# GLA state at token 256 in the lane of the levels, squares one step behind their matmuls, gate transfers tied to the second v product's first tile

## The chip, the cores and the metric

The kernel runs on one core of one Trainium2 chip. The metric is the device time of one execution in microseconds (us). The core has a matmul engine (TensorE, PE in the profile; PEld is its weight load), a vector engine (VectorE, DVE), a scalar engine (ScalarE, ACT), GpSimd (POOL) and SyncE (SP), which here only issues transfers. Each engine works through its own instructions in a fixed order; semaphores make one wait for another. Matmul results go to PSUM, in two pools of four banks here, called mm and px.

## The reference

One decoder layer on 512 tokens of width 1024, in float32: a layer norm; gated linear attention (GLA, 4 heads, keys of 128, values of 256) and latent attention side by side, each projected back; the two merged by sigmoid gates and projected; a norm; a squared-ReLU MLP of width 4096; a norm. The GLA part, which the change touches, is

```
q_g, k_g, v_g, r_g, a_lr, q_lat, kv_lat, gate_logits = jnp.split(h @ w_in, offsets, axis=-1)
log_a = jax.nn.log_sigmoid((a_lr @ w_gla_a2 + b_gla_a2).astype(jnp.float32)) / GLA_TAU
# S_t = diag(a_t) S_{t-1} + k_t^T v_t,  o_t = q_t S_t
o_gla = gla_chunked(q * GLA_HK ** -0.5, k, v, log_a)
o_gla = rms_norm(o_gla.transpose(0, 2, 1, 3), gla_norm_g.reshape(GLA_HEADS, GLA_HV))
y_gla = (o_gla * jax.nn.silu(r_g)) @ w_o_gla
g_gla, g_mla = jnp.split(jax.nn.sigmoid(gate_logits + b_gate), N_BRANCH, axis=-1)
return (g_gla * y_gla + g_mla * y_mla) @ w_out
```

## The kernel before

Every product in float32 is made of three matmuls: both operands are split into a high part (rounded, written by ACT) and a low part (the remainder, written by VectorE), and high x high, high x low and low x high are summed in PSUM. For weights the parts are whi and wlo, made by split (L191 on ACT, L192 on VectorE) from a tile of 512 KB. A tile comes in a buffer wraw (three of them, loaded on SP's queue at L176) or wq; whi and wlo have two buffers each. fetch, which issues L176, runs two tiles ahead of the products.

The products of the normed input run one after the other: q and k, v of heads 0 and 1 (proj_v(0)), r (proj_r, L752 to L754), v of heads 2 and 3 (proj_v(1), L281 to L283), then the gates (unit, L1222 to L1224). r and the gates use a scheme of fewer multiplications, for which some weight tiles are sums or differences of two source tiles: u_load issues one transfer on SP (L1195) and, for the sums, a second one on POOL (L1197) that adds to the tile where it lies. The first six gate tiles (wq of "g0": two each of "t1", "22", "t3") are called for ahead of proj_v(1). The gates also read shifted inputs sh (L1282, 16 transfers on SP).

Between the matmuls of these products runs the work of GLA, in generators (lanes) that a product moves on by a step at a time (tick). lane_levels runs gla_levels for head 0, 1, 2, 3. A head's scores are built level by level (blocks of 2, 4, ... 256 tokens): decays makes the decay factors dec (ACT L781 and L787) from sums gs that POOL makes (L785), M is packed by ACT (L811), L851, L867, L870 and L874 are its matmuls into px, and SD collects the scores; sd, s128 and s256 are the split results. lane_out runs gla_out for each head, once SS[h] (the levels), Vh[h] (the split v, vh and vl) and four blocks of r (rg) are there: first the state at token 256, the sum of k^T v over the first 256 tokens, six matmuls of 128x256 (L906 to L908), and its split over the same s256 tile; then for four blocks i of 128 tokens the output (L928 to L930): three matmuls for each of the terms, two blocks to a px bank; then the square of each block with its row sum (osq, gss; ACT L932), the root on POOL (grs L937), the scaling by rg (og L942) and transposes (L948).

The order that each engine gets is not the order of the code: a scheduler of the language works on recorded instructions (schedule_with_timeline_sim in L1693), and tc.issue_after tells it that instructions may stand only behind a given one. Names in the rows below are those of the program; a number behind a name tells one buffer from another.

Of the kernel before, what the change touches and what calls it, by code (L numbers as in the profile page):

```python
# [10 lines left out]
F32 = mybir.dt.float32  # L11
# [4 lines left out]
AF = mybir.ActivationFunctionType  # L16
# [3 lines left out]
P = 128  # L20
T = 512
D = 1024
NT = T // P
# [3 lines left out]
GH = 4  # L27
HV = 256
# [24 lines left out]
def tile_hybrid_block(ctx: ExitStack, tc: tile.TileContext, I, out, dbg=None):  # L53
    nc = tc.nc
# [11 lines left out]
    def nm(s):  # L66
        uid[0] += 1
        return f"{s}_{uid[0]}"
# [4 lines left out]
    def A(shape, dt=F32, n="a"):  # L73
        tag, bufs = ("C", 8) if n in TAG_C else (n, TAG_W[n]) if n in TAG_W else ("A", 24)
        return pa.tile(shape, dt, tag=tag, bufs=bufs, name=nm(n))

    def B(shape, dt=F32, n="b"):
        return pb.tile(shape, dt, tag="B", name=nm(n))

    def S(shape, dt=F32, n="s"):  # L80
        return sm.tile(shape, dt, tag=n, name=nm(n))
# [8 lines left out]
    def PX(shape=(P, T), dt=F32, n="px"):  # L90
        return px.tile(list(shape), dt, tag="px", name=nm(n))

    def f(ap):
        return ap.bitcast(F32)

    act = nc.scalar.activation
# [12 lines left out]
    def split(src, hi, lo, scale=None):  # L109
        if scale is None:  # L110
            act(hi, src, AF.Copy)
            return vtt(lo, src, f(hi), op=ALU.subtract)
        else:
            act(hi, src, AF.Copy, scale=scale)
            return stt(lo, src, scale, f(hi), op0=ALU.mult, op1=ALU.subtract)
# [23 lines left out]
    stream = []  # L139
# [24 lines left out]
    def fetch(n):  # L164
        while st["dma"] < min(len(stream), n):
            e = stream[st["dma"]]
            st["dma"] += 1
            if "src" in e:
                continue
            raw = A([P, e["nk"], T * 2 // e["nk"]], F32, "wraw")  # L170
            for sl, src, cw in e["dmas"]:
                if cw is None:
                    dst = raw[:, sl, :e["n"]]
                else:
                    dst = raw[:, sl[0], sl[1]].rearrange("p (h c) -> p h c", c=cw)
                nc.sync.dma_start(dst, src)  # L176
            e["raw"] = raw

    def pump(i):
# [122 lines left out]
    PL = {}  # L302
# [16 lines left out]
    for op, _ in RW:  # L319
        for hf in range(2):  # L320
            PL["r"].append(len(stream))
            e = {"nk": 2, "n": T, "res": False, "ahead": 2, "home": "wwwwrwrwrwwwrw"[2 * RW.index((op, _)) + hf]}
# [24 lines left out]
    def u_src(key, i, j, g):  # L347
        name, c0, gs = UNITS[key]
        src = I[name].rearrange("(k p) n -> p k n", p=P)
        c0 += (j * gs + g) * 256  # L350
        return src[:, i:8:2, c0:c0 + 256]
# [312 lines left out]
    Vh = [None] * GH  # L664
# [24 lines left out]
    rgn = [0] * GH  # L689
# [84 lines left out]
    SS = [None] * GH  # L774
# [119 lines left out]
        split(p[:, :256].rearrange("p (t i) -> p t i", i=P), sd[:, 0, 2:], sd[:, 1, 2:])  # L894
        SS[h] = (sd, s128, s256)

    def gla_out(h):
        while SS[h] is None or Vh[h] is None or rgn[h] < NT:
            yield
        sd, s128, s256 = SS[h]  # L900

        vh, vl = Vh[h]
        p = PX()[:, :HV]
        for j in range(2):
            kh, kl = [s256[:, 0, w, j * P:(j + 1) * P] for w in range(2)]
            mm(p, kh, vh[:, j, :], start=j == 0, stop=False)  # L906
            mm(p, kh, vl[:, j, :], start=False, stop=False)
            mm(p, kl, vh[:, j, :], start=False, stop=j == 1)  # L908
        sh, sl = s256[:, 0, 0], s256[:, 0, 1]
        split(p, sh, sl)  # L910

        def terms(i):
            if i % 2:
                yield (s128[:, 0, i // 2], s128[:, 1, i // 2]), (vh[:, i - 1, :], vl[:, i - 1, :])
            yield (sd[:, 0, i], sd[:, 1, i]), (vh[:, i, :], vl[:, i, :])
            if i >= 2:
                c = slice((i - 2) * P, (i - 1) * P)
                yield (s256[:, 1, 0, c], s256[:, 1, 1, c]), (sh, sl)

        ss = S([P, NT], F32, "gss")  # L920
        ps = []
        for i in range(NT):
            if i % 2 == 0:
                ps.append(PX())
            o = ps[i // 2][:, (i % 2) * HV:(i % 2 + 1) * HV]
            ts = list(terms(i))
            for n, ((ah, al), (wh, wl)) in enumerate(ts):
                mm(o, ah, wh, start=n == 0, stop=False)  # L928
                mm(o, ah, wl, start=False, stop=False)
                mm(o, al, wh, start=False, stop=n == len(ts) - 1)  # L930
            sq = B([P, HV], F32, "osq")
            act(sq, o, AF.Square, accum_out=ss[:, i:i + 1])  # L932
            if i >= 1:
                yield
        vts(ss, ss, 4.0 / HV, 4.0 * RMS_EPS, op0=ALU.mult, op1=ALU.add)
        rs = S([P, NT], F32, "grs")
        gtt(rs, ss, mhalf[:, :NT], op=ALU.pow)  # L937
        yield
        og = [B([P, 2, HV], F32, "og") for _ in range(2)]
        for i in range(NT):  # L940
            o = ps[i // 2][:, (i % 2) * HV:(i % 2 + 1) * HV]
            stt(og[i // 2][:, i % 2, :], o, rs[:, i:i + 1], Rg[h][:, i, :], op0=ALU.mult, op1=ALU.mult)  # L942
        yield
        for kk in range(2):
            k = 2 * h + kk
            p = PX()
            for tt in range(NT):
                nc.tensor.transpose(p[:, tt * P:(tt + 1) * P], og[tt // 2][:, tt % 2, kk * P:(kk + 1) * P], ident)  # L948
            yield
            o = A([P, 2, T], F32R, "ogT")  # L950
            split(p, o[:, 0, :], o[:, 1, :], scale=glg[:, k:k + 1])
            ogT[k] = o
# [193 lines left out]
    def lane_levels():  # L1146
        for h in range(GH):
            yield from gla_levels(h)
            lv[h] = True

    def lane_out():
        for h in range(GH):
            yield from gla_out(h)

    t_lv, t_out = spawn(lane_levels()), spawn(lane_out())

    def levels_upto(h):
# [34 lines left out]
    def u_load(key, op, dma=nc.sync.dma_start):  # L1192
        for g in range(UNITS[key][2]):
            t = WQ[key, (op, g)] = A([P, 4, 256], F32, "wq")
            dma(t, u_src(key, *{"21": (1, 0), "22": (1, 1)}.get(op, (0, 1)), g))  # L1195
            if op[0] == "t":
                nc.gpsimd.dma_start(t, u_src(key, *{"t1": (0, 0), "t3": (1, 1)}[op], g), accum_op=ALU.add)  # L1197
# [85 lines left out]
                hops[p][ph] = (t[:, 0], t[:, 1])  # L1283
            yield

    u_load("g0", "t1")
    u_load("g0", "22")
    u_load("g0", "t3")
    def g_start():
        levels_upto(1)  # L1290
        spawn(h_load())
# [59 lines left out]
    t1, mv = mla_pair(1)  # L1351
# [3 lines left out]
    t3, mv = mla_pair(3)  # L1355
# [136 lines left out]
    def win_f2(ci, hid):  # L1492
        bank = {}
        for n, (op, hf, ph) in enumerate(WIN):
# [37 lines left out]
            if ci == FC - 2 and n == U2:  # L1532
                fetch(PL["f1", "22", 0] + 1)
# [163 lines left out]
```

## Time and profile before

| | us |
|---|---|
| median of 3 runs (882.39 to 882.45) | 882.4 |
| the profiled execution | 881.44 |
| its span | 879.6 |
| TensorE granted clock, mean | 0.995 |
| ACT busy, share of the span | 53% |
| POOL busy, share of the span | 16% |

The span is what the profile covers of the execution, from its first to its last instruction; 1.84 us lie around it. An engine's busy time is the time in which it executes; a wait is idle time with what ended it behind an arrow. The page cuts the span into 40 slices of 22 us. The stretch that the change reorders is the sixth to the twelfth:

```profile
PE   5999999989999999999999999999999999999996
POOL 1323305210100030300000013004400520141000
DMA  7995947796627443322207537007931990499312
```

A digit is a busy share in tenths; for DMA it is the mean of the core's 16 transfer engines.

### The profile page before, as it was taken

The page shows a single profiled execution, that of the slowest core. Times are in us where ns is not written, and L with a number is a line of the kernel's source. Part 1 is how long each engine was busy: PE and PEld are TensorE (multiplying, and loading weights), DVE is VectorE, ACT ScalarE, POOL GpSimd, SP SyncE. Part 2 cuts the span into 40 slices and gives each one's busy share as a digit, 9 for nine tenths or more (in the row PEclk, how much of TensorE's full clock was granted, in tenths as well). Part 3 has the DMA queues.
Part 4 walks back from the last instruction along what each step waited for, and adds up shares of the span by engine and source line. Part 5 has one row for each costly group of instructions (what it writes and reads, how often), then busy time and mean ns, then how long its engine had stood idle before and what let it go on. Part 6 is the DMA issues. An engine that isn't in the chain of part 4 may idle for free.

```text
span 879.6 us, 12827 instructions
## 1 busy us (share of the span) xinstructions
PE 857.2 (97%) x4757; PEld 747.1 (85%) x4757; DVE 632.8 (72%) x1045; ACT 470.1 (53%) x829; POOL 144.8 (16%) x184
## 2 busy tenths in 40 slices
PE   5999999989999999999999999999999999999996
PEld 5988888878989978888888889988888888889985
DVE  7859989858665646657766788886567646788865
ACT  6456777555555624435545414576357446656820
POOL 1323305210100030300000013004400520141000
PEclk9999999999999999999999999999999999999998
DMA  7995947796627443322207537007931990499312
GB/s 250 284 222 150 329 144 175 222 226 197 163 84 175 147 132 93 102 67 72 79 33 276 172 91 268 1 0 201 278 96 43 264 244 25 91 232 233 118 63 78
DMA packets 95215, 134.58 MB, mean 153 GB/s; under 512 B 12673, under 2 KB 58113, under 8 KB 95153
## 3 DMA queue, kind: packets, MB, share of 16 engines
q1 hardware_dynamic: 73840, 92.36, 33.1%
q0 software_dynamic: 19392, 37.76, 19.9%
q10 hardware_dynamic: 1920, 3.66, 1.1%
q8 instruction: 37, 0.61, 0.3%
q14 instruction: 26, 0.20, 0.1%
HBM read 110.15 MB, written 8.91 MB: 135 GB/s over the span
## 4 chain that ended last, share of the span: by engine, by line
PE 93%; DVE 3%; DMA 2%; ACT 1%; issue 1%; SPq 0%; POOLq 0%; POOL 0%; DVEq 0%; ACTq 0%
PE mm L247 11%; PE mm L248 11%; PE mm L249 11%; PE mm L283 5%; PE mm L282 5%; PE mm L281 5%; PE mm L1224 4%; PE mm L1223 4%; PE mm L1222 4%; PE px L1508 2%; PE px L1509 2%; PE px L1510 2%; DMA wraw<-in_w_in_dram 2%; PE mm L1508 2%; PE mm L1509 2%; PE mm L1510 2%
## 5 line engine op out<-in xcount | busy, mean ns | idle before, releaser
L192 DVE TENSOR_TENSOR wlo<-wraw,whi 128x1024 fp32r<-128x1024 f32 (+1 forms) x90 | 99.1, 1102 | 97.2 <-ACT whi L191 90.8
L191 ACT ACTIVATE whi<-wraw 128x1024 fp32r<-128x1024 f32 (+1 forms) x90 | 85.5, 950 | 95.3 <-PE mm L248 42.2
L248 PE MATMUL mm<-h,whi 128*128 128x512 f32 x224 | 87.3, 390 | 0.0
L247 PE MATMUL mm<-h,whi 128*128 128x512 f32 x224 | 87.2, 390 | 0.0
L249 PE MATMUL mm<-h,wlo 128*128 128x512 f32 x224 | 83.3, 391 | 0.0
L192 DVE TENSOR_TENSOR wlo<-wq,whi 128x1024 fp32r<-128x1024 f32 x44 | 53.9, 1225 | 31.6 <-ACT whi L191 31.6
L1527 POOL DMA_DIRECT2D res<-ev x42 | 37.4, 1018 | 180.0 <-ACT ev L1525 145.8
L191 ACT ACTIVATE whi<-wq 128x1024 fp32r<-128x1024 f32 x44 | 46.5, 1057 | 32.6 <-PE mm L1223 20.0
L1224 PE MATMUL mm<-sh,wlo 128*128 128x256 f32 x176 | 50.0, 284 | 0.0
L1222 PE MATMUL mm<-sh,whi 128*128 128x256 f32 x176 | 50.0, 284 | 0.0
L1223 PE MATMUL mm<-sh,whi 128*128 128x256 f32 x176 | 49.9, 283 | 0.0
L249 PEld LDWEIGHTS mm<-h,wlo 128*128 128x128 f32 x224 | 42.0, 188 | 9.1 <-DVE wlo L192 0.4
L247 PEld LDWEIGHTS mm<-h,whi 128*128 128x128 f32 x224 | 42.1, 188 | 8.7
L248 PEld LDWEIGHTS mm<-h,whi 128*128 128x128 f32 x224 | 42.1, 188 | 8.6
L191 ACT ACTIVATE xh<-wraw 128x1024 fp32r<-128x1024 f32 (+1 forms) x28 | 27.4, 986 | 27.4 <-PE mm L283 15.4
L192 DVE TENSOR_TENSOR xl<-wraw,xh 128x1024 fp32r<-128x1024 f32 (+1 forms) x28 | 31.3, 1130 | 8.9 <-ACT xh L191 8.9
L1570 ACT ACTIVATE relu<-mm 128x512 f32<-128x512 f32 x24 | 14.1, 595 | 42.0 <-PE mm L249 42.0
L1222 PEld LDWEIGHTS mm<-sh,whi 128*128 128x128 f32 x176 | 33.8, 192 | 0.0
L1223 PEld LDWEIGHTS mm<-sh,whi 128*128 128x128 f32 x176 | 33.8, 192 | 0.0
L1224 PEld LDWEIGHTS mm<-sh,wlo 128*128 128x128 f32 x176 | 33.8, 192 | 0.0
L1224 PE MATMUL mm<-h,wlo 128*128 128x256 f32 x112 | 31.8, 286 | 1.3 <-DVE wlo L192 1.3
L1222 PE MATMUL mm<-h,whi 128*128 128x256 f32 x112 | 32.1, 287 | 0.8 <-ACT whi L191 0.8
(495 smaller groups left out, 2700.5 us busy)
## 6 DMA issues: line engine op xcount, KB each, us to landing
wraw<-in_w_ff_dram SPq DMA_DIRECT2D x36, 512.0 KB, 4.9
wraw<-in_w_in_dram SPq DMA_DIRECT2D x30, 512.0 KB, 4.9
wq<-in_w_ff_dram POOLq DMA_DIRECT2D x26, 512.0 KB, 9.6
res<-ev POOLq DMA_DIRECT2D x42, 256.0 KB, 10.3
wq<-in_w_in_dram SPq DMA_DIRECT2D x20, 512.0 KB, 6.7
wq<-in_w_in_dram POOLq DMA_DIRECT2D x18, 512.0 KB, 10.1
hsd<-hs SPq DMA_DIRECT2D x16, 256.0 KB, 4.3
xr<-hsd SPq DMA_DIRECT2D x16, 256.0 KB, 5.0
```

Source lines behind the costliest of these rows:

```text
L191: st["ins"] = act(hi[:, :nk, :n], raw[:, :nk, :n], AF.Copy)
L192: st["lo"] = vtt(lo[:, :nk, :n], raw[:, :nk, :n], f(hi[:, :nk, :n]), op=ALU.subtract)
L247: mm(o, hi[:, c], xh, start=first, stop=False)
L248: mm(o, hi[:, c], xl, start=False, stop=False)
L249: mm(o, lo[:, c], xh, start=False, stop=last)
L281: mm(o, xh, hi[:, :n], start=opens, stop=False, skip_group_check=share)
L282: mm(o, xh, lo[:, :n], start=False, stop=False, skip_group_check=share)
L283: mm(o, xl, hi[:, :n], start=False, stop=last, skip_group_check=share)
L1222: mm(oa, hi[:, k, c], xh, start=opens and k == 0 and a == 0, stop=False, skip_group_check=True)
L1223: mm(oa, hi[:, k, c], xl, start=False, stop=False, skip_group_check=True)
L1224: mm(oa, lo[:, k, c], xh, start=False, stop=k == 3, skip_group_check=True)
L1527: nc.gpsimd.dma_start(res[tt + t][:, j * T:(j + 1) * T], e, accum_op=ALU.add)
```

## The change

Three edits. First, the state's matmuls and split leave gla_out for a generator of their own, gla_state, which lane_levels runs behind the levels of heads 0 and 1, and behind all levels for heads 2 and 3; gla_out waits for its flag. Second, in gla_out the squares of blocks 0 and 1 are issued together once block 1's matmuls are issued, and a step of the lane (yield) comes between a block's matmuls and its square. Third, the transfers of the first six gate tiles stand in an issue_after of the transfer of the second v product's first tile. Lines behind L893 move by up to 15.

```
-                nc.sync.dma_start(dst, src)
+                e["dma"] = nc.sync.dma_start(dst, src)
...
-    def gla_out(h):
-        while SS[h] is None or Vh[h] is None or rgn[h] < NT:
-            yield
-        sd, s128, s256 = SS[h]
-
-        vh, vl = Vh[h]
-        p = PX()[:, :HV]
+    ST = [False] * GH
+
+    def gla_state(h):
+        while Vh[h] is None:
+            yield
+        s256, (vh, vl), p = SS[h][2], Vh[h], PX()[:, :HV]
         for j in range(2):
             kh, kl = [s256[:, 0, w, j * P:(j + 1) * P] for w in range(2)]
             mm(p, kh, vh[:, j, :], start=j == 0, stop=False)
             mm(p, kh, vl[:, j, :], start=False, stop=False)
             mm(p, kl, vh[:, j, :], start=False, stop=j == 1)
+        yield
+        split(p, s256[:, 0, 0], s256[:, 0, 1])
+        ST[h] = True
+
+    def gla_out(h):
+        while not ST[h] or rgn[h] < NT:
+            yield
+        sd, s128, s256 = SS[h]
+
+        vh, vl = Vh[h]
         sh, sl = s256[:, 0, 0], s256[:, 0, 1]
-        split(p, sh, sl)
...
-            sq = B([P, HV], F32, "osq")
-            act(sq, o, AF.Square, accum_out=ss[:, i:i + 1])
             if i >= 1:
                 yield
+                for n in (0, 1) if i == 1 else (i,):
+                    sq = B([P, HV], F32, "osq")
+                    act(sq, ps[n // 2][:, (n % 2) * HV:(n % 2 + 1) * HV], AF.Square, accum_out=ss[:, n:n + 1])
...
             yield from gla_levels(h)
             lv[h] = True
+            if h < 2:
+                yield from gla_state(h)
+        for h in (2, 3):
+            yield from gla_state(h)
...
-    u_load("g0", "t1")
-    u_load("g0", "22")
-    u_load("g0", "t3")
+    with tc.issue_after(stream[PL["v", 1]["idx"][0]]["dma"].ins):
+        u_load("g0", "t1")
+        u_load("g0", "22")
+        u_load("g0", "t3")
+
```

**The gate transfers on SP and POOL.** On SP, after the change, around the first two tiles of the second v product (the first and the last wraw of these rows) the program has:

```order
L176 DMA wraw_1837<-in_w_in_dram 128x2x512
L1208 DMA wq_1910<-in_w_in_dram 128x4x256
L1208 DMA wq_1913<-in_w_in_dram 128x4x256
L1208 DMA wq_1916<-in_w_in_dram 128x4x256
L1208 DMA wq_1918<-in_w_in_dram 128x4x256
L1208 DMA wq_1920<-in_w_in_dram 128x4x256
L1208 DMA wq_1923<-in_w_in_dram 128x4x256
L176 DMA wraw_1865<-in_w_in_dram 128x2x512
```

Before, the same eight stand there in the same order (with L1195 for L1208). On POOL, the chain of sums gs of head 3 and the accumulating transfers of the gate tiles stand, before the change, like this:

```order
L785 TENSOR_TENSOR gs_1775<-gs_1775 128x64
L785 TENSOR_TENSOR gs_1775<-gs_1775 128x32
L785 TENSOR_TENSOR gs_1775<-gs_1775 128x16
L785 TENSOR_TENSOR gs_1775<-gs_1775 128x8
L785 TENSOR_TENSOR gs_1775<-gs_1775 128x4
L1197 DMA wq_1903<-in_w_in_dram 128x4x256
L1197 DMA wq_1906<-in_w_in_dram 128x4x256
L888 TENSOR_TENSOR sd_1937<-SD_1662,sd_1937 128x256
L1197 DMA wq_1913<-in_w_in_dram 128x4x256
```

and after it like this:

```order
L785 TENSOR_TENSOR gs_1822<-gs_1822 128x64
L1210 DMA wq_1910<-in_w_in_dram 128x4x256
L785 TENSOR_TENSOR gs_1822<-gs_1822 128x32
L1210 DMA wq_1913<-in_w_in_dram 128x4x256
L785 TENSOR_TENSOR gs_1822<-gs_1822 128x16
L785 TENSOR_TENSOR gs_1822<-gs_1822 128x8
L785 TENSOR_TENSOR gs_1822<-gs_1822 128x4
L1210 DMA wq_1920<-in_w_in_dram 128x4x256
L888 TENSOR_TENSOR sd_2006<-SD_1724,sd_2006 128x256
```

SP's order has not moved; on POOL two of the accumulating transfers now stand inside the chain.

**The state and the squares.** On TensorE, before, the state of head 0 (L906 to L908) stands in the first tile of the second v product (whi_1863 and wlo_1864):

```order
L281 MATMUL mm_1929<-whi_1863,h_12_116 128x512
L892 MATMUL px_1945<-ca,SD_1662 128x128 x2
L906 MATMUL px_1948<-vh_1341,s_281_1370 128x256
L907 MATMUL px_1948<-vl_1342,s_281_1370 128x256
L908 MATMUL px_1948<-vh_1341,s_281_1370 128x256
L906 MATMUL px_1948<-vh_1341,s_281_1370 128x256
L907 MATMUL px_1948<-vl_1342,s_281_1370 128x256
L908 MATMUL px_1948<-vh_1341,s_281_1370 128x256
L282 MATMUL mm_1925<-wlo_1864,h_12_116 128x512
```

After, it (L905 to L907 now) stands in the second tile of the r product (whi_1302); two of its six:

```order
L752 MATMUL mm_1378<-whi_1302,h_24_148 128x512
L752 MATMUL mm_1391<-whi_1302,h_24_148 128x512
L905 MATMUL px_1384<-vh_1341,s_281_1370 128x256
L906 MATMUL px_1384<-vl_1342,s_281_1370 128x256
L851 MATMUL px_1432<-x_291_1415,x_290_1413 128x192 x2
L753 MATMUL mm_1378<-wlo_1303,h_24_148 128x512
L754 MATMUL mm_1378<-whi_1302,h_24_148 128x512
```

The other four follow behind ten matmuls of the r product, and head 1's six stand later in the same product, where none of it stood. On ACT, before, around the split of the second v tile (whi_1921):

```order
L111 ACTIVATE s_281_1370<-px_1948 128x256
L932 ACTIVATE osq_1962,gss_1957<-px_1958 128x256
L191 ACTIVATE whi_1921<-wraw_1861 128x1024
L191 ACTIVATE whi_2019<-wraw_1919 128x1024
L932 ACTIVATE osq_1970,gss_1957<-px_1958 128x256
```

and after (whi_1928):

```order
L943 ACTIVATE osq_1980,gss_1949<-px_1950 128x256
L943 ACTIVATE osq_1982,gss_1949<-px_1950 128x256
L111 ACTIVATE s_425_2009<-px_1974 128x256
L191 ACTIVATE whi_1928<-wraw_1865 128x1024
L943 ACTIVATE osq_2017,gss_1949<-px_1984 128x256
```

Blocks 0 and 1 are squared side by side ahead of the split, and block 2 behind it; the state's split (s_281 from px_1948) is gone from here.

**The tiles of the gates.** On TensorE, before, the last rows of one gate tile (whi_2697) are followed by six of gla_out and then by the first rows of a tile whose input is h (whi_2783):

```order
L1223 MATMUL mm_2300<-sh_2393,whi_2697 128x256
L1224 MATMUL mm_2300<-sh_2393,wlo_2698 128x256
L928 MATMUL px_2607<-vh_2258,s_478_2286 128x256
L929 MATMUL px_2607<-vl_2259,s_478_2286 128x256
L930 MATMUL px_2607<-vh_2258,s_478_2286 128x256
L928 MATMUL px_2607<-vh_2258,sd_2307 128x256
L929 MATMUL px_2607<-vl_2259,sd_2307 128x256
L930 MATMUL px_2607<-vh_2258,sd_2307 128x256
L1222 MATMUL mm_2446<-h_15_124,whi_2783 128x256
L1223 MATMUL mm_2446<-h_15_124,whi_2783 128x256
```

After, the same tile (whi_2692) is followed by another gate tile on sh (whi_2736):

```order
L1236 MATMUL mm_2289<-sh_2391,whi_2692 128x256
L1237 MATMUL mm_2289<-sh_2391,wlo_2693 128x256
L1235 MATMUL mm_2354<-sh_2385,whi_2736 128x256
L1236 MATMUL mm_2354<-sh_2385,whi_2736 128x256
L1237 MATMUL mm_2354<-sh_2385,wlo_2737 128x256
```

That tile's 24 matmuls run to their end, and the tile on h comes behind them; before, it came ahead of them.

## The prediction

> **What bounds the kernel now.** I read the page first, then the waits of TensorE, then short windows and timelines around each wait that the change can reach. TensorE is the bound:
>
> ```profile
> PE 857.2 (97%) x4757; PEld 747.1 (85%) x4757; DVE 632.8 (72%) x1045; ACT 470.1 (53%) x829; POOL 144.8 (16%) x184
> ```
>
> It is busy for 857.2 of 879.6 us. The change keeps every matmul and only reorders them, so only TensorE's idle time, and time in which it runs slowly, can be won or added. The list of TensorE's waits says where its idle time lies:
>
> ```profile
> PE mm L281 <- ACT whi L191: 2.7, 1, 2.7
> PE mm L1224 <- DVE wlo L192: 1.3, 2, 0.8
> PE px L928 <- ACT osq L932: 1.1, 1, 1.1
> PE mm L1222 <- ACT whi L191: 0.8, 2, 0.5
> ```
>
> The only longer wait of the list is at the start of the kernel, which the change does not touch. These four, 5.9 us together, lie between 177 and 257 us, in the stretch that the change reorders. The timeline shows the largest, at the second tile of the second v product:
>
> ```profile
> 177.36 0.28 PE L930 MATMUL px<-vh,sd 128*128 128x256 f32 x1
> 180.38 1.21 PE L281 MATMUL mm<-whi,h 128*128 128x512 f32 x4 [2.74 <-ACT whi L191]
> 181.64 0.56 PE L282 MATMUL mm<-wlo,h 128*128 128x512 f32 x1
> ...
> 185.39 0.39 PE L282 MATMUL mm<-wlo,h 128*128 128x512 f32 x1
> 185.62 0.39 PE L283 MATMUL mm<-whi,h 128*128 128x512 f32 x1
> ```
>
> After 2.74 us of idling, matmuls of 128x512 start 0.43 us apart until 185.39, instead of 0.23 us (185.39 to 185.62). From 181.64 to 185.39 are nine of them: 3.75 us instead of 2.07. The four before took 1.26 instead of 0.92. So the stall has a tail of 1.7 + 0.3 = 2.0 us. The windows show that the tail is the granted clock (the number behind POOL's busy time):
>
> ```profile
> 177.30:180.40 3.10, 0.36 (x4) 0.16 (x3) 0.04 (x1) 1.06 (x1) 0.90 (x1) 1.00 1.14 276
> 180.40:185.30 4.90, 4.85 (x13) 3.58 (x14) 3.63 (x7) 3.07 (x7) 0.00 (x0) 0.66 1.19 244
> 204.00:210.00 6.00, 4.82 (x39) 4.40 (x38) 6.00 (x18) 5.78 (x19) 0.38 (x1) 1.00 0.76 238
> 243.00:257.00 14.00, 11.89 (x93) 11.10 (x93) 7.86 (x13) 8.68 (x19) 1.04 (x1) 1.00 0.01 1
> ```
>
> The clock is 0.66 on average behind the stall, and 1.00 around the shorter waits of the other two windows. The same windows price these: 1.2 us idle of 6.0, and 2.1 of 14.0.
>
> What the stall waits for stands in the chain of waits:
>
> ```profile
> 165.78 13.47 DMA wraw<-in_w_in_dram
> 179.27 1.06 ACT whi L191
> ```
>
> The second weight tile of the product takes 13.47 us to land, then 1.06 us on ACT. It was issued behind the first tile and six gate transfers on the same queue:
>
> ```profile
> 160.19 0.38 SPq L176 DMA_DIRECT2D wraw<-in_w_in_dram  x1
> 160.66 4.97 SPq L1195 DMA_DIRECT2D wq<-in_w_in_dram  x6
> 165.78 3.13 SPq L176 DMA_DIRECT2D wraw<-in_w_in_dram  x3
> ```
>
> **Change, part 1: the hold.** It does nothing by itself. In the program of before, SP already issues the first v tile, the six gate tiles and the second v tile in this order, and it does after. It removes no transfer between the two v tiles. Term: 0.
>
> **Part 2: the state at token 256 moves.** The six matmuls of head 0 leave the first tile of the second v product for the r projection ahead of it, those of head 1 leave the end of that product for the r projection too. They start 0.12 us apart (rows 205.19 and 205.31 below), 0.7 us per head. Head 0's were and are ahead of the stalled tile: nothing. Head 1's now come ahead of it, so TensorE asks for the tile 0.7 us later. Other matmuls of the chain move too, and one small bubble is added:
>
> ```profile
> 121.34 1.47 PE L851 MATMUL px<-x,x 128*128 128x192 f32 x8
> 122.51 0.53 PE L752 MATMUL mm<-whi,h 128*128 128x512 f32 x1
> 121.82 1.08 DVE L112 TENSOR_TENSOR vl<-mm,vh 128x256 fp32r<-128x256 f32 x3
> ```
>
> The state needs vl from VectorE (two of the three done at about 122.5), and the L851 group that covers the time until then is now behind it. Half of that group, 0.6 us, would have to be waited for; bounds 0 and 0.6, I take **+0.4**, since small gaps elsewhere close. TensorE then asks for the second tile at 177.5 + 0.7 = 178.2 us.
>
> **Part 3: when that tile now lands.** The train starts when VectorE has read an older tile of the three-buffer ring:
>
> ```profile
> 158.94 1.22 DVE L192 TENSOR_TENSOR wlo<-wraw,whi 128x1024 fp32r<-128x1024 f32 x1
> ```
>
> It ends at 160.16, and SP issues at 160.19. In the new order this split stands directly behind two sums of the r product (er) and one short row of the scores, ahead of the mask rows that it followed before. The sums wait for TensorE:
>
> ```profile
> 148.60 1.46 PE L851 MATMUL px<-x,x 128*128 128x192 f32 x8
> 154.22 0.60 PE L867 MATMUL px<-M 128*128 128x128 f32 x4
> 155.13 0.39 PE L754 MATMUL mm<-whi,xr 128*128 128x512 f32 x1
> 156.19 0.68 DVE L726 TENSOR_TENSOR er<-er,mm 128x512 f32<-128x512 f32 x1
> ```
>
> Their last matmul ends at 155.5 now. Ahead of it go both states (+1.4); behind it go the L851 group (1.2, from 148.60 to 149.76) and an L867 group (0.36); plus the bubble of 0.4: 155.7. Then 0.7 for the sum, 0.4 for the score row and 1.2 for the split: 158.0, that is 2.1 us earlier than 160.16. SP's six gate tiles and the accumulating transfers on POOL start as much earlier. The second v tile is still issued at about 166 (its buffer is read by TensorE until then), with the queue full, so it lands when the queue has got to it: 179.25 - 2.1 = 177.2. ACT ends at 178.2 + 0.1. The stall falls from 2.74 us to **about 0.3** (bounds 0 and 2.2, rival A), and the slow clock behind it goes: **-2.4 and -2.0**.
>
> The idle of 1.06 us at 205.31 had no slow clock behind it, that of 2.74 had one; where between them it begins no row shows. The Trainium skill ("TensorE: Matmul & The Clock Gate", Part 1: The HAM clock gate) says that the clock halves after at least one idle window of about 3.4 us, and that these windows run freely. By the rule taken literally 2.74 us would not have halved it; the trace shows that it did, for about the length of one such window. By the page's free phase, a stall left at 1 to 2 us could cost 2.0 us more in one run and nothing in another; by the trace alone it costs nothing up to 1.06.
>
> **Part 4: squares a step behind.** The waits they can remove:
>
> ```profile
> 205.19 0.28 PE L929 MATMUL px<-vl,sd 128*128 128x256 f32 x1
> 205.31 0.28 PE L930 MATMUL px<-vh,sd 128*128 128x256 f32 x1
> 206.65 0.39 PE L928 MATMUL px<-vh,s 128*128 128x256 f32 x1 [1.06 <-ACT osq L932]
> ```
>
> The second row block writes the bank that ACT's square still reads; 1.2 us is lost. With the squares of blocks 0 and 1 issued together, this wait is gone. The next pair's first square is now one that TensorE needs (block 3 writes the bank of block 2), and in head 0 it stands on ACT behind the tile that stalled. There TensorE has four matmuls (0.92 us) before it asks; the square and its readout need less:
>
> ```profile
> L932 ACT ACTIVATE osq<-px x16: 364/384/426, 173.3 to 250.1; 128x256 f32<-128x256 f32 x16
> L932 ACT ACTIVATION_READ_ACCUMULATOR osq<-px x16: 191/194/253, 173.5 to 250.4; 128x1 f32 x16
> ```
>
> 0.38 + 0.19 = 0.58 us (the middle number is the median in ns): covered. At the v-to-gate border the mask chain of head 3 now ends later; it can give back all of it. Bounds -1.2 and +0.5; I take **-0.7**.
>
> **Part 5: order of the gate tiles.** In the kernel before, the tile at 245.22 runs ahead of the one that was loaded before it:
>
> ```profile
> 245.22 0.38 PE L1222 MATMUL mm<-h,whi 128*128 128x256 f32 x1 [0.31 <-ACT whi L191]
> 246.48 0.38 PE L1224 MATMUL mm<-h,wlo 128*128 128x256 f32 x1 [0.76 <-DVE wlo L192]
> ```
>
> whi and wlo have two buffers each: this tile's halves cannot be made until TensorE has left the tile two before it, and only six short matmuls (0.7 us) lie between, while ACT needs 1.06 and DVE 1.22. After, the 24 matmuls of the other tile (24 x 0.12 = 2.9 us) lie between. Both this pair of waits and the next like it lose their cause, 1.3 + 0.8 = 2.1 us by the list of waits, which has two of each. ACT and DVE have the delayed state splits there too. Bounds -2.1 and +0.5; I take **-1.6**.
>
> **Sum.** +0.4 - 2.4 - 2.0 - 0.7 - 1.6 = -6.3 us. The profiled execution took 881.44 us (span 879.6 and 1.84 around it): 875.1. The median of the runs is 0.96 above the profiled one: **876.1 us**, with 874.4 if all of them go and no bubble is added (873.8 if small gaps of 0.6 close beside them), and 878.3 if half of the last three terms fails.
>
> **Rivals.**
> *A: the second v tile lands no earlier.* POOL's accumulating transfers now start with the train and take their share:
>
> ```profile
> 150.89 3.68 POOL L785 TENSOR_TENSOR gs<-gs 128x128 f32<-128x128 f32 x6
> 166.01 2.71 POOL L1197 DMA_DIRECT2D wq<-in_w_in_dram  x2 [11.44 <-DMA wq<-in_w_in_dram]
> ...
> 176.91 1.28 POOL L1197 DMA_DIRECT2D wq<-in_w_in_dram  x1 [3.10 <-DMA wq<-in_w_in_dram]
> ```
>
> If it still lands at 179.25, the stall is 179.25 + 1.1 - 178.2 = 2.2 us and the clock falls again: -0.6 + 0.4 - 0.7 - 1.6 = -2.5, 878.9 + 0.96 = **879.9**. For it: the DMA share around the stall is above 1 in the window's rows (1.14 and 1.19). Against it: all of the train moves by the same 2.1 us. The Trainium skill ("DMA: Bandwidth & Descriptors", Issuing engines are not separate DMA queues) says that transfers of all issuing engines run on the same 16 engines and interleave, which speaks for A; by it as by the trace, the bytes ahead of the tile decide.
>
> *B: the stalls move.* The tile lands late as in A, and the new chain order gives back what parts 4 and 5 gain (0 for both): -0.6 + 0.4 = -0.2, **882.2**. For it: ACT and DVE are 96 and 100% busy between 204 and 210.
>
> *C, slower: POOL's queue blocks ACT.* The accumulates of the first two gate tiles now stand inside head 3's gs chain, which was done at 154.57 (150.89 + 3.68) without waiting for a gate tile. After, its last three rows (3.68 / 6 = 0.6 us each) wait for the second gate tile to land and for its issue. That tile had landed when its accumulate was issued, half of 2.71 us behind 166.01, at 167.4; 2.1 earlier is 165.3. ACT's dec waits for the chain:
>
> ```profile
> L787 ACT ACTIVATE dec<-gs x4: 610/620/629, 95.2 to 162.3; 128x508 f32<-128x508 f32 x4
> ```
>
> Behind dec, in ACT's own order, stand nine rows of 0.4 to 0.6 us, some 4.5, and then the split of the second v tile: ready at 165.3 + 1.3 + 1.8 + 0.6 + 4.5 = 173.5, while the v tile lands at 177.2. It decides if the gate tile lands after 169. If that came at 176.9, as late as the last one that POOL waits for now, the split would begin at 185.1 and the stall be 185.1 + 1.1 - 178.2 = 8.0 us: +5.3 with the clock as now, + 0.4 - 0.7 - 1.6 gives +3.4, 884.8 + 0.96 = **885.8**. Against it: the copies are first in SP's queue and far ahead of that.
>
> **How the numbers follow.** Forecast 0.57, A 0.14, B 0.15, C 0.14. The range reaches from the forecast's best, 873.8, over A and B and a third of the way from B's end to C: 873.8 to 884.0; what lies above is most of C, about 0.1. A measurement of this kernel can tell 0.2%, 1.8 us, from no change: below 880.6 is faster. Faster: the forecast and two thirds of A, 0.66. Within: B and a third of A, 0.20. Slower: 0.14.
>
> **What would show it.** Right: the wait of L281 for whi under 0.7 us, the granted clock 1.00 behind it, the wraw transfer of part 3 issued by 158.5 and the next landing by 177.5; no wait of 1 us on osq; no pair of waits of L1222 and L1224 at about 240 to 252. Wrong: the same wait over 2 us with a clock near 0.66 (A or B), or a dec on ACT after 172 with the split right behind it (C). The prediction fails most likely in the landing time, where 1.5 us decide over the slow clock.

## The result, and the profile after

| | before | changed |
|---|---|---|
| median of 4 runs each on one chip, us | 882.42 (882.39 to 884.82) | 875.67 (874.96 to 875.98) |
| ratio, 95% interval | | 0.9916 (0.9898 to 0.9933) |
| profiled execution, us | 881.44 | 874.96 |
| its span, us | 879.6 | 873.2 |
| TensorE granted clock, mean | 0.995 | 0.998 |

The kernel is 0.84% faster: 6.5 us between the two profiled executions, 6.75 between the medians. The page's row of busy times, for the changed kernel:

```profile
PE 854.5 (98%) x4757; PEld 746.0 (85%) x4757; DVE 634.0 (73%) x1045; ACT 470.7 (54%) x829; POOL 144.0 (16%) x184
```

The span fell by 6.4 us. TensorE executes the same 4757 matmuls; its idle time fell from 879.6 - 857.2 = 22.4 to 873.2 - 854.5 = 18.7 us, and its busy time by 2.7. So 3.7 us are waits that went, and 2.7 are matmuls that ran in less time. The list of TensorE's waits of the changed kernel (in total, times, longest, in us) says which waits are left:

```profile
PE px L446 <- ACT x L435: 8.9, 1, 8.9
PE mm L752 <- DVE vl L112: 0.9, 1, 0.9
PE mm L281 <- ACT whi L191: 0.8, 1, 0.8
...
PE mm L1235 <- ACT u L1251: 0.2, 1, 0.2
```

Of the four waits of before, osq (1.1) and the pairs of the gates (1.3 and 0.8) are gone, and 0.8 of 2.7 us is left at L281. One wait is new: 0.9 us of L752 for vl, and there is a small one of L1235. The first row is the start of the kernel. The same stretches as in the prediction, as windows of the changed kernel (after the length: busy us of PE, PEld, DVE, ACT and POOL, then granted clock, DMA share and GB/s):

```profile
180.00:185.00 5.00, 4.17 (x25) 3.59 (x24) 3.78 (x4) 4.68 (x12) 0.00 (x0) 1.00 1.17 259
204.00:210.00 6.00, 6.00 (x48) 5.82 (x47) 4.96 (x15) 4.72 (x12) 1.34 (x2) 1.00 0.48 153
243.00:257.00 14.00, 14.00 (x120) 14.00 (x119) 10.09 (x15) 9.43 (x22) 1.04 (x1) 1.00 0.24 62
```

The clock behind the rest of the stall is 1.00 where it was 0.66, and TensorE is busy without a gap in the two other windows, where it had been idle for 1.2 and 2.1 us. TensorE's timeline shows the two waits that remain in the reordered stretch (in brackets the idle time ahead of a row and what ended it):

```profile
121.85 0.38 PE L892 MATMUL px<-ca,SD 128*128 128x128 f32 x2
123.11 0.47 PE L752 MATMUL mm<-whi,h 128*128 128x512 f32 x1 [0.88 <-DVE vl L112]
...
181.01 1.20 PE L281 MATMUL mm<-whi,h 128*128 128x512 f32 x4 [0.82 <-ACT whi L191]
```

At 121.85 the L851 group that stood there before has moved on, and nothing covers VectorE's vl.

### The profile page after: what moved, and what is told of

It is laid out like the page before. It is cut to its first block, busy times and chain, and to the rows that moved or that the text cites. A ratio compares the mean times of both kernels' runs of the same rounds, so it can differ in the third digit from the quotient of the medians.

```text
span 873.2 us, 12830 instructions
## 1 busy us (share of the span) xinstructions
PE 854.5 (98%) x4757; PEld 746.0 (85%) x4757; DVE 634.0 (73%) x1045; ACT 470.7 (54%) x829; POOL 144.0 (16%) x184
## 4 chain that ended last, share of the span: by engine, by line
PE 95%; DMA 2%; DVE 1%; ACT 1%; issue 0%; POOLq 0%; SPq 0%; DVEq 0%; ACTq 0%
PE mm L247 11%; PE mm L248 11%; PE mm L249 11%; PE mm L283 5%; PE mm L281 5%; PE mm L282 5%; PE mm L1235 4%; PE mm L1236 4%; PE mm L1237 4%; PE px L1524 2%; PE px L1523 2%; PE px L1525 2%; PE mm L1524 2%; PE mm L1523 2%; PE mm L1525 2%; PE mm L752 1%
## 5 line engine op out<-in xcount | busy, mean ns | idle before, releaser
L1235 PE MATMUL mm<-sh,whi 128*128 128x256 f32 x176 | 50.0, 284 | 0.2 <-ACT u L1251 0.2
L1235 PEld LDWEIGHTS mm<-sh,whi 128*128 128x128 f32 x176 | 33.8, 192 | 0.4 <-ACT u L1251 0.4
L1235 PE MATMUL mm<-h,whi 128*128 128x256 f32 x112 | 31.9, 285 | 0.0
```

The source lines that it names most:

```text
L1235: mm(oa, hi[:, k, c], xh, start=opens and k == 0 and a == 0, stop=False, skip_group_check=True)
```

## The experiments

Twelve kernels ran, each beside the kernel before on the same chip. Ratios are to the runs of that kernel beside it, with 95% intervals. Two questions stood open: which of the three edits carries the gain, and why the stall at L281 shrank although its tile did not land sooner.

**The state's move alone.** Of the change, only the move of the state and its flag are kept:

```
-    with tc.issue_after(stream[PL["v", 1]["idx"][0]]["dma"].ins):
...
-                for n in (0, 1) if i == 1 else (i,):
-                    sq = B([P, HV], F32, "osq")
-                    act(sq, ps[n // 2][:, ...], AF.Square, accum_out=ss[:, n:n + 1])
+            sq = B([P, HV], F32, "osq")
+            act(sq, o, AF.Square, accum_out=ss[:, i:i + 1])
```

> The state in the levels' lane alone; squares and gate transfers as before. Theory (the stall at the second v tile shrinks because TensorE reaches the tile later, with head 1's state and a new bubble of about 0.9 us ahead of it, while the transfers keep their times): wait of L281 for whi 0.5 to 1.2 us with a granted clock of 1.00 behind it, the wait of L752 for vl 0.9 us, the waits at the gates (L1222 and L1224 for whi and wlo, 2.1 us in the kernel before) still there: 882.4 - 1.9 - 2.0 + 1.1 = 879.6 us. Rival (the squares' edit thins out the work around the tile and so ends the stall): wait of L281 above 2 us and a clock near 0.66, about 883.

Measured: median 881.34, ratio 0.9988 (0.9976 to 0.9999). Its list of TensorE's waits:

```profile
PE px L446 <- DMA wraw<-in_w_in_dram: 9.1, 1, 9.1
PE mm L1236 <- DVE wlo L192: 2.0, 2, 1.3
PE mm L1234 <- ACT u L1250: 0.9, 1, 0.9
PE mm L752 <- DVE vl L112: 0.9, 1, 0.9
PE px L936 <- ACT osq L940: 0.8, 2, 0.6
...
PE px L867 <- ACT vh L111: 0.5, 1, 0.5
...
PE mm L1234 <- ACT whi L191: 0.3, 1, 0.3
```

The stall at L281 and its slow clock are gone, 2.7 + 2.0 = 4.7 us; from 180 to 200 us TensorE is busy throughout, at a clock of 1.00. But the gates' waits grew from 2.1 to 2.0 + 0.9 + 0.3 = 3.2, vl costs 0.9, vh 0.5, and the start of this execution 0.7 (9.1 instead of 8.4). So the move ends the largest wait and gives most of it back in others. The expectation had the clock and the wait for vl right; the stall of 0.5 to 1.2 us did not come, and 879.6 us was too low, since it left the waits at the gates as they were.

**The squares alone.** The kernel before with the second edit only:

```
-            sq = B([P, HV], F32, "osq")
-            act(sq, o, AF.Square, accum_out=ss[:, i:i + 1])
             if i >= 1:
                 yield
+                for n in (0, 1) if i == 1 else (i,):
+                    sq = B([P, HV], F32, "osq")
+                    act(sq, ps[n // 2][:, ...], AF.Square, accum_out=ss[:, n:n + 1])
```

> The squares a step behind alone; state and gate transfers as before. Theory: the wait of L281 stays at 2.5 to 2.9 us with the slow clock behind it, since the state is where it was; the waits on osq (1.1) and at the gates (2.1 us) are gone, because in this order the tile on h stands behind the other gate tile: 882.4 - 1.7 - 2.6 = 878.1 us. Rival (the gates' order comes from the state): gate waits of 2 us stay, about 880.7.

Measured: median 876.10, ratio 0.9925 (0.9907 to 0.9944). The longest wait of TensorE behind the start, then a window behind the stall:

```profile
PE mm L281 <- ACT whi L191: 2.6, 1, 2.6
```

```profile
181.00:190.00 9.00, 8.48 (x38) 6.84 (x38) 5.11 (x11) 3.58 (x10) 0.51 (x1) 0.81 1.17 264
```

The stall and the slow clock (0.81 over these 9 us) are as before, and still the time falls nearly as far as with the whole change: the osq wait and all waits of the gates are gone. The order of the gate tiles, which the prediction put down to the change as a whole, comes with this edit. What the state's move adds to it (0.9916 beside 0.9925) the intervals do not separate. The median is 2.0 us below the expected 878.1: besides 3.4 us of idle time, TensorE's busy time fell by 2.0 us, to 855.2, although the slow clock stayed. Where those 2.0 lie is open; the squares' edit also reorders other matmuls.

**The pair without the step.** The squares of blocks 0 and 1 issued together, but right behind block 1's matmuls, with the yield behind them:

```
             if i >= 1:
+                for n in (0, 1) if i == 1 else (i,):
+                    sq = B([P, HV], F32, "osq")
+                    act(sq, ps[n // 2][:, ...], AF.Square, accum_out=ss[:, n:n + 1])
                 yield
```

> The kernel before with one difference: the squares of blocks 0 and 1 are issued together behind block 1's matmuls, in the same step of the lane (no step between matmuls and squares). In the program the gate tile on h stands behind the other gate tile again, as with both halves of the edit. Theory (the pairing alone does it, since the wait on osq was for block 0's square between two blocks of one bank): no wait of 1 us on osq for the first pair, no pair of waits at the gates, the stall at the second v tile as before: about 877 us, ratio 0.993 to 0.995. Rival (the step between matmuls and squares does it): waits on osq of 1 us stay near 206 us, 879 to 881.

Measured: median 877.07, ratio 0.9945 (0.9923 to 0.9967). Waits of TensorE:

```profile
PE mm L281 <- ACT whi L191: 1.0, 1, 1.0
PE px L929 <- DVE s L112: 0.6, 1, 0.6
PE px L867 <- DVE ogT L115: 0.6, 1, 0.6
```

The pairing alone takes the osq wait and the gates' waits away; at the border 1.2 us come back as two other waits. In this order the stall is 1.0 us, not 2.7 as expected, and no slow clock follows it (1.00 from 180 to 200 us); why it is shorter was not followed up. The step without the pairing was not run.

**The hold taken away.** The changed kernel without the issue_after line. Every engine then has the same instructions in the same order as with it.

```
-    with tc.issue_after(stream[PL["v", 1]["idx"][0]]["dma"].ins):
```

> The changed kernel without the hold: the order on all five engines is the same row for row, so this is also the changed kernel timed beside the next three on one chip. Theory (the hold does nothing): the ratio to the kernel before is 0.9916 as measured for the changed kernel, within 0.15%, and the wait of L281 for whi 0.5 to 1.2 us. Rival (something that the order does not show depends on the hold): over 0.3% away.

Measured: median 874.95 (873.48 to 876.94), ratio 0.9909 (0.9894 to 0.9924): the hold does nothing. ACT's timeline, first of the changed kernel, then of this one, shows how far the same program varies:

```profile
179.91 1.06 ACT L191 ACTIVATE whi<-wraw 128x1024 fp32r<-128x1024 f32 x1 [2.42 <-DMA wraw<-in_w_in_dram]
```

```profile
179.42 1.06 ACT L191 ACTIVATE whi<-wraw 128x1024 fp32r<-128x1024 f32 x1 [1.46 <-DMA wraw<-in_w_in_dram]
```

The tile landed 0.5 us earlier here, and TensorE did not wait at L281. The stall left by the change is 0 to 0.8 us, by the execution.

**The hold on a later tile.** Gate transfers behind the second v tile, on the kernel before and on the changed one, with the fetch that this needs:

```
+    fetch(PL["v", 1]["idx"][1] + 1)
+    with tc.issue_after(stream[PL["v", 1]["idx"][1]]["dma"].ins):
```

> The kernel before with one difference: the six gate transfers stand behind the transfer of the second v tile on SP, not only behind the first. Theory (the tile is late because of the six ahead of it): it lands about 9 us earlier, by 171, the wait of L281 for whi and the slow clock go: 882.4 - 2.7 - 2.0 = 877.7 us, if the gates have slack for transfers that land some 2 us later. Rival (the gates have none): a new wait at the first gate tile on sh of 1 us and more gives it back, 879 to 882.

> The changed kernel with the hold one tile further: the six gate transfers behind the second v tile. Theory: the rest of the stall (0.8 us) goes and nothing else moves by more than 0.3: 875.7 - 0.8 = 874.9 us. Rival (the third v tile is now late): a wait of L281 for whi of 1 us and more at the third tile, near 187 us, 875.5 to 877.

Measured: on the kernel before 883.29, ratio 1.0016 (1.0003 to 1.0028); on the changed kernel 876.71, ratio 0.9934 (0.9915 to 0.9952). In the second the rival came. In the first the second tile landed early, as the theory had it, but neither its time nor that of the rival came; the timelines of ACT and TensorE show that the stall has moved by one tile, from the second to the third:

```profile
170.51 1.07 ACT L191 ACTIVATE whi<-wraw 128x1024 fp32r<-128x1024 f32 x1
187.44 1.06 ACT L191 ACTIVATE whi<-wraw 128x1024 fp32r<-128x1024 f32 x1 [7.26 <-DMA wraw<-in_w_in_dram]
```

```profile
188.55 2.07 PE L281 MATMUL mm<-whi,h 128*128 128x512 f32 x4 [3.98 <-ACT whi L191]
```

The second tile is split at 170.51, ready 6 us before TensorE asked for it in the kernel before (177.6); the third lands at 187.4. In the second kernel it waits as well, 1.5 us, without a slow clock behind it:

```profile
189.00:194.00 5.00, 4.49 (x21) 3.53 (x21) 3.63 (x8) 3.32 (x9) 1.41 (x1) 1.00 1.21 217
```

**The hold on the third tile,** with [2] for [1], on the changed kernel:

> The changed kernel with the six gate transfers behind the third v tile. In the run with the hold behind the second tile the third came late (1.5 us of waiting). Theory: second and third tile land ahead of the gate tiles, by 176, the fourth by 190 with TensorE asking for it near 194: no wait of L281 above 0.3 us, 875.7 - 0.8 = 874.9 us. Rival (the fourth tile takes its place): a wait of L281 of 1 us and more near 194 us, 875.5 to 877.

Measured: 874.23, ratio 0.9898 (0.9883 to 0.9914). No wait at L281 is left in its list; that for vl is.

**The state two steps later.** The states of heads 0 and 1 run inside the next head's levels, two steps in:

```
+            g = gla_levels(h)
+            if h in (1, 2):
+                for _ in range(2):
+                    next(g)
+                    yield
+                yield from gla_state(h - 1)
+            yield from g
```

> The changed kernel with the states of heads 0 and 1 two steps later in the lane, behind the first steps of the next head's levels, so that the L851 group of head 1 stands again ahead of the product's wait for vl. Theory 1 (the transfers to the second v tile hang on TensorE's own progress, by way of the ring of three wraw buffers): the wait for vl (0.9 us) goes, the tile lands as much earlier and the stall of L281 stays near 0.8: 875.7 - 0.9 = 874.8 us. Theory 2 (the transfers keep their times): TensorE reaches the tile 0.9 us earlier and waits 0.9 us longer, 1.7 us in all, 875.7 us.

Measured: 874.08, ratio 0.9899 (0.9885 to 0.9912). The wait for vl is gone, and 0.3 us are left at L281. The queue of SP in this kernel, and ACT's split of the tile ahead of the train:

```profile
152.21 7.22 SPq L176 DMA_DIRECT2D wraw<-in_w_in_dram  x2
159.52 5.01 SPq L1212 DMA_DIRECT2D wq<-in_w_in_dram  x6
```

```profile
155.90 1.06 ACT L191 ACTIVATE whi<-wraw 128x1024 fp32r<-128x1024 f32 x1
```

One issue takes 0.38 us, so the first v tile, the second of the two wraw, is issued at 152.21 + 7.22 - 0.38 = 159.05: 1.1 us earlier than in the kernel before. Here the train does move, in the direction that the prediction had for the change, by half of its 2.1 us. The first of the two theories came: without the wait for vl the stall did not grow, and the median is 0.9 below that of the kernel without the hold, run beside it (874.95), though their intervals overlap.

**The train made longer.** The changed kernel with a transfer of 512 KB that nothing uses, between the first v tile and the gate tiles, and then with two of them:

```
+        nc.sync.dma_start(DR([P, 1024], "pad"), I["w_in"][0:P, 0:1024])
```

> The changed kernel with one transfer more: 512 KB from DRAM to DRAM on SP between the first v tile and the six gate tiles; its output is used by nothing. Everything else keeps its order. The second v tile should land about 1.5 us later and the wait of L281 be 2.0 to 2.6 us. Theory (a wait of that length takes the clock down as the waits of 2.57 and 2.74 did): a half clock for about 3.4 us behind it, +1.5 + 1.7 us, 878 to 879 us in the profile. Rival (the clock goes down only above some 2.5 us or by where the wait falls): clock 1.00 behind it, about 876.5.

> The changed kernel with two transfers of 512 KB more between the first v tile and the six gate tiles, DRAM to DRAM, used by nothing. With one such transfer the wait of L281 was 1.27 us at a clock of 1.00; here 1.6 to 2.2 us. Theory (the clock falls behind a wait only where the wait fills most of one of its periods of 3.4 us, as 2.57 and 2.74 did and 1.50 did not): clock 1.00 still. Rival (a fixed length between 1.5 and 2.57 decides): half clock for 3.4 us behind it.

One run each: 875.25 with one, 878.48 with two. Both sizes were missed. The rows of L281, with one and with two:

```profile
181.37 1.20 PE L281 MATMUL mm<-whi,h 128*128 128x512 f32 x4 [1.27 <-ACT whi L191]
```

```profile
183.16 1.80 PE L281 MATMUL mm<-whi,h 128*128 128x512 f32 x4 [3.83 <-ACT whi L191]
```

The wait is 0.4 us longer with one (1.27 beside 0.82) and 3.0 longer with two. The wait also depends on when TensorE asks, so the landing is better counted from the issue of the first v tile to ACT's split of the second. That is 18.6 to 20.2 us in the seven kernels here with the train as before (the kernel before, the changed one, and those with the state alone, the squares alone, the pair, no hold and the late state), 20.3 with one added transfer and 23.1 with two. So the two transfers did delay the tile, to 2.9 us above the longest of the seven; the effect of one is no larger than the scatter without any. With two, some of TensorE's order differs as well, which was not separated.

**Combinations.** The late state with the hold on the third tile, and the squares with the hold on the third tile but the state left where it was:

> Both single improvements together: states two steps later in the lane, gate transfers behind the third v tile. Theory (each removes its own loss): no wait for vl, no wait of L281 above 0.2 us; ratio to the kernel before about 0.989 - 0.0005 = 0.9885. Rival (with TensorE 0.9 us earlier the fourth v tile comes late): a wait of L281 of 0.5 us and more near 192 us, ratio 0.990.

> The squares a step behind, with the state where it was in the kernel before and the gate transfers behind the third v tile. Theory (all that the state's move brings is the end of the stall at the second v tile, which the hold ends as well, without the wait for vl): no wait of L281 above 0.3 us, clock 1.00 throughout, 876.1 - 2.6 - 1.8 = 871.7 us, ratio 0.988 to 0.989. Rival 1 (the fourth v tile comes late, TensorE being 2.6 us earlier there): a wait of 1 us and more near 190 us, 873 to 876. Rival 2 (the state's move also frees the border to the gates): waits on osq or vl of 1 us near 205 us.

Measured: 873.60, ratio 0.9904 (0.9887 to 0.9921), and 872.78, ratio 0.9892 (0.9872 to 0.9912). In the first, the waits for vl and at L281 are gone as expected, but the ratio is no better than with either alone (0.9899 and 0.9898). The waits of the second:

```profile
PE px L446 <- ACT x L435: 9.2, 1, 9.2
PE px L1225 <- DVE wlo L192: 0.8, 1, 0.8
```

Its second row lies at 786 us, far behind the change; between 100 and 300 us no wait of the list is left. It has the lowest median of all, without moving the state. The intervals of the two, of the late state and of the change overlap, so which of them is fastest stays open; that the state's move isn't needed is shown.

## Why the prediction was right, point by point

| term | forecast | measured | by |
|---|---|---|---|
| bubble at vl | +0.4 | +0.9 | wait of L752 |
| stall at L281 | -2.4 | -1.9 | 2.74 to 0.82 |
| slow clock | -2.0 | -2.0 | clock 0.66 to 1.00 |
| osq | -0.7 | -1.2 | window 204 to 210 |
| gates | -1.6 | -1.9 | window 243 to 257, less the 0.2 of L1235 |
| sum | -6.3 | -6.1 | profiled executions: -6.5 |

The total was right, partly by luck. Errors of both signs met: the stall and the bubble came out 1.0 worse, osq and gates 0.8 better. And the two largest terms, 4.4 of the 6.3 us, came by another way than the working said (part 3). The start of the kernel took 0.5 more (8.9 instead of 8.4); against that and the -6.1, some 0.9 us of the -6.5 are spread over pieces too small for these views. Of the signs that the prediction set for being right, three did not come: the stall under 0.7 us (0.82), the issue by 158.5 (160.24) and the landing by 177.5 (179.9). The clock of 1.00 and the end of the waits on osq and at the gates did.

**Part 1, the hold: right.** The kernel without it is the same program and has the same time.

**Part 2, the bubble: right in kind, mis-sized.** The upper bound, 0.6, was that half of the L851 group; the wait is 0.88. The group's place was priced, but not the whole way of vl through ACT and VectorE behind the product's end.

**Part 3, the landing: this step failed.** It said that the train starts 2.1 us earlier. The queue of SP in the changed kernel:

```profile
153.45 7.17 SPq L176 DMA_DIRECT2D wraw<-in_w_in_dram  x2
160.71 5.11 SPq L1208 DMA_DIRECT2D wq<-in_w_in_dram  x6
168.19 17.30 SPq L176 DMA_DIRECT2D wraw<-in_w_in_dram  x5
```

The first v tile went out at 153.45 + 7.17 - 0.38 = 160.24, as before (160.19), not at 158.0; and the second landed at 179.9, not at 177.2. Two things were missing from the working, which counted TensorE's matmuls up to the sums er and let the split follow them. The first is TensorE itself. The last matmul of those sums, at 155.13 in the kernel before, stands in the changed kernel at

```profile
156.69 0.39 PE L754 MATMUL mm<-whi,xr 128*128 128x512 f32 x1
```

It ends at 157.1, where the working had 155.7. Of these 1.4 us, the bubble gives 0.5 (0.88 instead of 0.4), and 0.7 stood already at 121 us, ahead of the reordered matmuls (121.85 beside 121.12 for the same row of L892), most of it from the start of this execution. The second is that the split which frees the buffer hangs on two other engines, in their own order. ACT in the kernel before, then in the changed one:

```profile
149.20 1.06 ACT L191 ACTIVATE whi<-wraw 128x1024 fp32r<-128x1024 f32 x1 [1.70 <-DMA wraw<-in_w_in_dram]
```

```profile
150.95 0.60 ACT L760 ACTIVATE er<-mm 128x512 f32<-128x512 f32 x1
151.70 1.06 ACT L191 ACTIVATE whi<-wraw 128x1024 fp32r<-128x1024 f32 x1
...
157.89 1.06 ACT L191 ACTIVATE whi<-wraw 128x1024 fp32r<-128x1024 f32 x1 [1.64 <-DMA wraw<-in_w_in_dram]
```

VectorE in the changed kernel:

```profile
152.79 1.23 DVE L192 TENSOR_TENSOR wlo<-wraw,whi 128x1024 fp32r<-128x1024 f32 x1 [1.03 <-ACT whi L191]
...
157.29 1.27 DVE L726 TENSOR_TENSOR er<-er,mm 128x512 f32<-128x512 f32 x2
158.48 0.41 DVE L859 TENSOR_TENSOR SD<-px,ca 128x256 f32<-128x256 f32 x1
158.98 1.23 DVE L192 TENSOR_TENSOR wlo<-wraw,whi 128x1024 fp32r<-128x1024 f32 x1
```

VectorE makes wlo of an earlier tile at 152.79, behind ACT's split at 151.70 (150.43 and 149.20 before), and shows no idle time between its rows from there on. So the second er sum starts only at 157.9, 0.8 us after its matmul, and the sums end at 157.29 + 1.27 = 158.6 instead of the 156.4 of the working: 1.4 us by TensorE and 0.8 by VectorE's queue behind it; how long the queue would have held them had TensorE been in time is open. ACT's split at 151.70 stands behind the two er rows, which followed it before. But its order alone is not shown to be the cause: by the order of SP's queue, the tile's load was issued at 147.73 instead of 145.17, 0.1 us behind TensorE's last read of an older buffer in both kernels, and from issue to split it is 4.0 us in both.

The split behind the sums would have waited for ACT in any case: its whi (157.89) waits for a landing, since that load too was issued 1.5 us later (153.45; 151.93 before). The row ahead of the split ends at 158.48 + 0.41 = 158.9 and whi at 157.89 + 1.06 = 158.95, so either alone would have held it. The kernel with the late state supports the part of VectorE's queue. TensorE's last matmul of the sums and VectorE's second sum there:

```profile
154.63 0.39 PE L754 MATMUL mm<-whi,xr 128*128 128x512 f32 x1
```

```profile
157.22 0.67 DVE L726 TENSOR_TENSOR er<-er,mm 128x512 f32<-128x512 f32 x1
```

TensorE is done at 155.0, earlier than the working had it, and the sum starts 2.2 us later, while ACT's whi of the split behind it is ready at 155.90 + 1.06 = 157.0; so VectorE's own queue held it. The train goes out 1.1 us ahead of before, not 2.1 or more. That experiment moves several things at once, so it does not price each of them.

That the stall shrank nevertheless has another cause: TensorE comes later. It asks for the tile at 181.01 - 0.82 = 180.2, instead of 180.38 - 2.74 = 177.6. Of these 2.55 us, 0.7 are there at 121 us as said above, 0.9 are the bubble and 0.7 head 1's state; 0.2 stay open. So in this execution most of what the stall lost was paid elsewhere, and what the move gained is the slow clock. The bubble was not needed for that: without it, in the kernel with the late state, the tile could be split at 178.0 and the stall was 0.3.

**Part 4, osq: right, and more than forecast.** The border gave nothing back in this kernel. **Part 5, the gates: right;** the squares alone bring it.

**The rivals.** A came half true, in that the tile lands no earlier (179.9), yet the stall it priced at 2.2 us was 0.8, for the reason above. Its ground, that the bytes ahead of the tile decide, is borne out only for the two added transfers. B did not come: both gains stayed. C did not come; its dec runs on ACT in the changed kernel at

```profile
171.20 0.61 ACT L787 ACTIVATE dec<-gs 128x508 f32<-128x508 f32 x1
```

and the split of the v tile, at 179.91, had waited 2.42 us for its transfer and not for this row.

## What to carry to other kernels

When a transfer's start is forecast from a ring of buffers, follow every engine that touches the buffer, in its own order: here the working from the bound engine's matmuls said 2 us earlier, and the issue did not move: these matmuls came 1.4 us later than worked out, and VectorE's queue added 0.8. A wait that vanishes may have been filled by a new one ahead of it, so compare when the bound engine asks, not only how long it waits. And do the parts alone: the small edit, two squares behind one another, carried nearly all of the gain, and the large one gave most of its own back.

## What the hardware showed unexpectedly

**The clock after a wait.** Windows of 180 to 200 us, for the kernel before (wait 2.74 us), two added transfers (3.83), the hold on the second tile without the change (3.98) and with it (1.50):

```profile
180.00:200.00 20.00, 19.57 (x92) 16.39 (x93) 14.67 (x27) 11.68 (x28) 1.04 (x1) 0.91 0.80 193
```

```profile
180.00:200.00 20.00, 16.84 (x82) 14.63 (x83) 14.60 (x29) 11.90 (x26) 1.96 (x2) 0.91 0.93 243
```

```profile
180.00:200.00 20.00, 16.02 (x71) 13.55 (x70) 10.45 (x18) 8.37 (x19) 3.61 (x3) 0.83 1.00 244
```

```profile
180.00:200.00 20.00, 17.96 (x94) 14.57 (x93) 11.79 (x25) 9.49 (x23) 3.99 (x3) 1.00 1.16 269
```

The lowest window of the third of these, from 188.5 to 192 us, had a clock of 0.50. With half clock, 0.91 means 0.09 x 20 x 2 = 3.6 us of it, and 0.83 means 6.8, about twice as long. Among TensorE's waits between 175 and 210 us, it came behind all four of 2.57 us and more (2.57, 2.74, 3.83 and 3.98), and behind none of 1.50 or less (0.82, 1.0, 1.06, 1.27 and 1.50). The longest wait is an exception: behind the 8.4 us at the start of the kernel before, the same column shows 1.00:

```profile
8.00:20.00 12.00, 11.14 (x58) 9.65 (x59) 11.33 (x25) 10.31 (x19) 1.02 (x2) 1.00 0.79 268
```

The Trainium skill ("TensorE: Matmul & The Clock Gate", Part 1: The HAM clock gate) has windows of about 3.4 us that run freely; the lengths of 3.6 and 6.8 us agree with one and two of them, but its condition of at least one idle window does not fit the waits of 2.57 and 2.74. Between 1.50 and 2.57 no run here shows where it begins. Whether the slow clock comes in every execution of the kernel before is open, too. Of its 42 executions beside the experiments, nine have a mean clock of 0.998 or more, with a median of 880.9 us, and the other 33 a median of 882.9. But that mean also counts the end of the span, where the clock of the kernel before is 0.50 from 875 us on, behind its last matmul, and those executions left no trace.

**One program, several landings.** With the same order on every engine, the second v tile's split could begin at 179.91 in one execution and at 179.42 in another, 19.7 and 18.9 us after the issue of the first v tile, and the wait at the start of the kernel lay between 8.4 and 9.4 us over these kernels' profiles (9.4 with the hold on the second tile of the changed kernel). A stall under 1 us, forecast from landings, is within that scatter.
